# First attention pair projected before the gated part's u, wider spacing of attention pieces, squares taken from copies

## The chip, the cores and the metric

The kernel runs on one core of one Trainium2 chip. The metric is the device time of one execution in microseconds (us), as a median over runs. The core has a TensorE (matrix multiplication, in the profile PE, its weight loads PEld), a VectorE (DVE), a ScalarE (ACT), a GpSimd (POOL) and a SyncE (SP), on whose queue all loads and stores of this kernel are issued.

## The reference, cut to what matters

Two transformer blocks over 512 tokens of width 1024 in fp32: a gated delta network with a squared-ReLU MLP, and then a block whose mixer has three parts side by side. The change lies in the mixer of the second block.

```python
hn = rms_norm(h, norm1_g)
proj = hn @ w_in
a_b, a_c, a_h, q, k, v, c_u, c_v = split(proj, ...)          # 3x256, 3x512, 2x256
y_a = a_b * short_conv(a_c * a_h, conv_w)                    # gated convolution
q = rms_norm(q by head, q_norm_g); k = rms_norm(k by head, k_norm_g)   # 8 heads of 64
y_b = stick_breaking_attention(q, k, v)
y_c = gelu(c_u) * (tril(w_s) @ rms_norm(gelu(c_v)) + b_s)    # gated part, chunks of 128
h = h + concat(y_a, y_b, y_c) @ w_out
...
def stick_breaking_attention(q, k, v):                       # for each block of 128 queries
    z = q @ k.T * scale
    log_rem = where(causal, log_sigmoid(-z), 0)
    suffix = cumsum(log_rem, reverse=True) - log_rem
    o = where(causal, exp(log_sigmoid(z) + suffix), 0) @ v
```

After it come a squared-ReLU MLP and a gate with a per-layer embedding.

## The kernel before, in words

Activations lie feature-major: 128 features on the partitions, 512 tokens along the row, 8 such tiles for the width of 1024. A product in fp32 is made of three matmuls in a faster fp32 form (`mm3`, L198): the high part of the weights with the high and the low part of the activations, and the low part of the weights with the high part of the activations. Weights come in units of 128x1024 over SP's queue into two raw buffers; ScalarE makes the high part of a unit (L186) and VectorE the low part (L187). `plan` (L838) is the list of units in the order in which `take` asks for them, and two are always under way. A projection (`proj`) is 8 such triples into one PSUM tile of the two-buffer pool `mm`; all small products take theirs from the pool of six `g` buffers (`pg`).

TensorE's instructions stand in the order in which the program issues them; the instructions of the other engines are put into their queues by the scheduler of the language, except those that are pinned. The order on TensorE is made by the class `Mix`, a clock of estimated nanoseconds. Main work (projections) advances it by STEP = 655 a triple and calls `tick`, which issues each side piece (a Python generator) that has come due. A side piece gives back its own cost and the delay until it may be called again. `drain` issues all that is left, with nothing in between, and `wait` only sets the clock forward.

The mixer's stage runs so: c_v token-major (`token_major`, 256 columns); two units of c_u, whose GELU follows on ScalarE, and then a load of ScalarE's table with logarithm and exponential (pinned); the gated part (`sgu`) and the attention (`attend`) are added as sides; then the main work goes on with pair 0, 1 and 2 of q and k, V token-major, pair 3, and six projections of the gated convolution (`conv_part`); `drain`; and the output projection (L1153 on), whose TensorE work takes the attention's features last.

A pair is two heads, with one projection for q and one for k. `qk_pair` copies each to SBUF (L1120) and squares it (L1121), and adds `qk_norm`: 2500 later, sums over features on TensorE, a root on ScalarE and VectorE (L1003, L236 to L238), a way through DRAM to spread the roots over partitions (four DMAs), and 8000 after that, the scaling of q and k on VectorE (L1012). Only then is the pair `ready`. `attend` asks for that every 500, waits RD = 3500 and issues the three score pieces of each pair (`scores`, 512, 512 and 256 columns for each of the two heads). A score piece has the logits on TensorE (L1031, mask L1036), absolute value, exponential and logarithm on ScalarE (L1041 to L1043), a maximum, a running sum and a subtraction on VectorE (L1044 to L1046), and an exponential on ScalarE (L1047). One piece later its two heads are transposed on TensorE (`weights`, L1054), each copied by VectorE or ScalarE (L1057). The steps of `attend` follow each other PACE = 2370 apart, two for a score piece: one for each head. OD = 4500 after the transposes of a pair's third piece for its second head, the pair's output product (`attn_out`, L1067) falls due, half at a time. The last pair's output is in `drain`'s hands if the projections have ended by then.

Of the kernel before, what the change touches and what calls it, by code (L numbers as in the profile page):

```python
# [10 lines left out]
AF = mybir.ActivationFunctionType  # L11
# [12 lines left out]
UM = 5  # L24
UK = 3
WR = 2
PACE = 2370
OD = 4500
RD = 3500
HD = 4500  # L30
# [92 lines left out]
def tile_gdn_then_mix(ctx: ExitStack, tc: tile.TileContext, A: dict, out: bass.AP):  # L123
    nc = tc.nc
    ctx.enter_context(tc.manual_schedule(engines={mybir.EngineType.PE}))
    v, s, g, pe = nc.vector, nc.scalar, nc.gpsimd, nc.tensor
# [10 lines left out]
    mix = Mix()  # L137
# [10 lines left out]
    def us(name, shape=(P, T)):  # L148
        return up.tile(list(shape), F32, tag="us", name=name, bufs=US)
# [7 lines left out]
    def pmm(shape=(P, T), name="mm"):  # L157
        return psm.tile(list(shape), F32, tag="mm", name=name)

    def pg(shape=(P, 4, P), name="pg"):  # L160
        return psg.tile(list(shape), F32, tag="g", name=name)
# [16 lines left out]
    def wunit(ap, eng=v):  # L178
        n = ap.shape[1]
        raw = wp.tile([P, 1024], F32, tag="wr", name="wr", bufs=WR)  # L180
        nc.sync.dma_start(out=raw[:, :n], in_=ap)
        while stores:
            nc.sync.dma_start(**stores.pop(0))
        H = wp.tile([P, 1024], R, tag="wh", name="wh")
        L = wp.tile([P, 1024], R, tag="wl", name="wl")
        s.copy(H[:, :n], raw[:, :n])  # L186
        eng.tensor_tensor(out=L[:, :n], in0=raw[:, :n], in1=f(H[:, :n]), op=SUB)  # L187
        return H, L
# [15 lines left out]
    plan, asked = [], []  # L204

    def ask():
        while plan and len(asked) < 2:
            key = plan.pop(0)
            asked.append((key, wunit(A[key[0]][key[1]])))

    def take(*key):
        ask()
        k, w = asked.pop(0)
        assert k == key, (k, key)
        return w

    def proj(w_ap, xH, xL, order=range(KD), ps=None):
        H, L = w_ap
        ps = pmm() if ps is None else ps
        for i, k in enumerate(order):  # L220
            o = slice(k * P, (k + 1) * P)
            mm3(ps, H[:, o], L[:, o], xH[k], xL[k], i == 0, i == KD - 1)
            if i < KD - 1:
                mix.tick(STEP)
        mix.now += STEP
        ask()
        return ps

    def rsqrt(alloc, m, shape, pin=False):
        y0 = alloc("rs_y", shape)  # L230
        ln = s.activation(out=y0, in_=m, func=AF.Ln)
        if pin:
            tc.keep_in_program_order(ln)
        s.activation(out=y0, in_=y0, func=AF.Exp, scale=-0.5)
        t = alloc("rs_t", shape)
        v.tensor_tensor(out=t, in0=y0, in1=y0, op=MUL)  # L236
        v.scalar_tensor_tensor(out=t, in0=t, scalar=-0.5, in1=m, op0=MUL, op1=MUL)
        v.scalar_tensor_tensor(out=t, in0=t, scalar=1.5, in1=y0, op0=ADD, op1=MUL)  # L238
        return t
# [29 lines left out]
    def row_form(ps, lhs, rhs):  # L269

        for c in range(NC):
            pe.matmul(ps[32 * c:32 * c + 32], lhsT=lhs(c), rhs=rhs(c), start=True, stop=True)
        return ps
# [19 lines left out]
    def over(dst, d):  # L293
        n = dst.shape[0]
        nc.sync.dma_start(out=dst, in_=d.unsqueeze(0).to_broadcast([n] + list(d.shape)))
# [9 lines left out]
    def par(name, j=0, n=1):  # L305
        o, _ = _OFF[name]
        return prm[:, o + j:o + j + n]
# [285 lines left out]
    for m in range(31, 0, -1):  # L593
        w = 32 - m
# [226 lines left out]
    for m in range(KD):  # L821
        if m < 2:
            out_half(m, 1)
            ps = head2[m][1]
        else:
            ps = proj(wunit(A["wo"][m]), yH, yL)
# [5 lines left out]
    def mlp_plan(w1, w2):  # L832
        for half in range(2):
            plan.extend((w1, 16 * half + j) for j in range(16))
            plan.extend((w2, 4 * m + 2 * half + q) for m in range(KD) for q in range(2))

    mlp_plan("w1", "w2")
    plan += [("wcv", 0), ("wcv", 1)] + [("win2", i) for i in (0, 1, 8, 9, 10, 11, 12, 13)]  # L838
    plan += [("wv", i) for i in range(4)] + [("win2", 14), ("win2", 15)] + [("win2", 2 + i) for i in range(6)]
    plan += [("wo2", m) for m in range(KD)]  # L840
    mlp_plan("w3", "w4")
# [101 lines left out]
    def token_major(units, n, kper, fin, hook=lambda u, i: None):  # L943
        pv = [pmm((P, n), "ptm") if n == T and c < 2 else pg((P, n), "ptm") for c in range(NC)]
        for u, key in enumerate(units):
            H, L = take(*key)
            last = n == T and u == len(units) - 1
            for i in range(kper * NC):
                kk, c = (i % kper, i // kper) if last else (i // NC, (i + 2) % NC)
                k = u * kper + kk  # L950
                cs_ = slice(c * P, (c + 1) * P)
                o = slice(kk * n, kk * n + n)
                pe.matmul(pv[c], lhsT=uH[k][:, cs_], rhs=H[:, o], start=k == 0, stop=False)  # L953
                pe.matmul(pv[c], lhsT=uL[k][:, cs_], rhs=H[:, o], start=False, stop=False)  # L954
                pe.matmul(pv[c], lhsT=uH[k][:, cs_], rhs=L[:, o], start=False, stop=k == KD - 1)  # L955
                mix.tick(STEP * n // T)
                if i == kper * NC - 1:
                    ask()
                if k == KD - 1:
                    fin(c, pv[c])  # L960
                hook(u, i)
# [35 lines left out]
    def qk_norm(hp, qk, pcs):  # L997
        yield 0, SQ
        pss = pg((P, 2, P), "pss")
        for w in range(2):  # L1000
            row_form(pss[:, w], lambda c: bd[:, 48:80], lambda c: qk[:, w, c * P:(c + 1) * P])
        mq = us("mq", (P, 2, P))
        v.scalar_tensor_tensor(out=mq, in0=pss, scalar=1.0 / 64, in1=epsR.unsqueeze(1).to_broadcast([P, 2, P]), op0=MUL, op1=ADD)  # L1003
        rq = rsqrt(us, mq, (P, 2, P))
        d = dr.tile([NC, 2, 2, P], F32, name=f"rq_d{hp}")
        nc.sync.dma_start(out=d.rearrange("c e w i -> (c e) w i"), in_=rq[0:P:16])
        for e in range(2):
            for w in range(2):
                over(qk[64 * e:64 * e + 64, w].rearrange("p (c i) -> p c i", c=NC), d[:, e, w])
        yield 600, OQ  # L1010
        for w in range(2):
            v.scalar_tensor_tensor(out=qk[:, w], in0=pcs[w], scalar=(qg8, par("kg"))[w], in1=qk[:, w], op0=MUL, op1=MUL)  # L1012
        ready[hp] = (qk[:, 0], qk[:, 1])
        yield 0, 0
# [60 lines left out]
    def attend():  # L1075
        seq = [(hp, b2, e) for hp in range(4) for b2 in range(3) for e in range(2)]
        fly = []
        for i in range(len(seq) + LAG):
            cost = 0
            if i < len(seq) and seq[i][2] == 0:  # L1080
                hp, b2 = seq[i][:2]
                if b2 == 0:
                    while hp not in ready:
                        yield 0, 500
                    yield 0, RD
                fly += scores(*seq[i][:2])
                yield fly[-1][-1] * 5 // 3, GAP
            if i >= LAG:
                w = fly.pop(0)
                weights(*w)  # L1090
                cost += w[-1] * 5 // 6
                if w[1:3] == (2, 1):
                    mix.add(attn_out(w[0]), OD)
            yield cost, max((PACE if seq[min(i, len(seq) - 1)][2] else PACE - GAP) - cost, 300)

# [18 lines left out]
    def qk_pair(hp):  # L1114
        qk = k4("qk", shape=(P, 2, T))
        pcs = []
        for w in range(2):
            ps = proj(take("win2", 8 + 2 * hp + w), uH, uL)
            pc = um("pc")
            s.copy(pc, ps)  # L1120
            s.activation(out=qk[:, w], in_=ps, func=AF.Square)  # L1121
            pcs.append(pc)
            mix.tick(0)
        mix.add(qk_norm(hp, qk, pcs), 0)

    nrm = norms()
    token_major([("wcv", i) for i in range(2)], 256, 4, cv_done, lambda u, i: next(nrm) if (u, i) in ((0, 10), (1, 11)) else None)
    for m in range(2):
        ps = proj(take("win2", m), uH, uL)
        mix.tick(0)  # L1130
        t = um("t")
        v.tensor_tensor(out=t, in0=ps, in1=rcB, op=MUL)
        s.activation(out=cu[:, m], in_=t, func=AF.Gelu)
# [2 lines left out]
    mix.add(sg, next(sg)[1])  # L1136
    rc2 = uk("rc2")
    g.tensor_tensor(out=rc2, in0=rcB, in1=rcB, op=MUL)
    mix.add(attend())
    qk_pair(0)  # L1140
    qk_pair(1)
    qk_pair(2)
    token_major([("wv", i) for i in range(4)], 512, 2, v_done)
    done.add("V")
    qk_pair(3)
    conv_part(0)
    conv_part(1)
    mix.drain()
# [4 lines left out]
    for m in range(KD):  # L1153
        scale_h(m)
        ps = proj(take("wo2", m), yH, yL, (0, 1, 6, 7, 2, 3, 4, 5))
# [20 lines left out]
    for m in range(KD):  # L1176
# [11 lines left out]
        if m < KD - 1:  # L1188
            ps = proj(take("wg", m), uH, uL, ps=pg((P, T), "mm") if m < 2 else None)
# [4 lines left out]
        for c in (slice(0, 256), slice(256, 512)):  # L1194
            ps = pmm((P, 256), "mmh")
# [98 lines left out]
```

## Time and profile before

| | |
|---|---|
| Median of 3 runs | 1284.78 us (1284.68 to 1289.81) |
| Profiled execution | 1285.04 us |
| Its span | 1282.9 us, 16468 instructions |
| PEld | 1039.4 us (81%) |
| DVE | 733.9 us (57%) |
| ACT | 545.6 us (43%) |
| POOL | 118.2 us (9%) |
| DMA | 132.07 MB, mean 103 GB/s |

The span is the time from the first to the last profiled instruction. Shares are busy time over the span. TensorE's matmuls are pipelined: a matmul's row is longer than the distance to the next one's start (0.39 against 0.23 us for 512 columns), so TensorE's pace is read from starts, and an idle time is counted only where nothing was in flight. TensorE's clock was granted in full in all 40 slices of the page.

### The profile page before, as it was taken

What the parts mean: (1) busy time and instruction counts of PE and PEld (TensorE: products, weight loads), DVE (VectorE), ACT (ScalarE), POOL (GpSimd) and SP (SyncE); (2) the same over time, 40 slices, a digit from 0 to 9 for tenths busy, and PEclk for the clock granted to TensorE, in tenths of its full rate; (3) what the DMA queues carried; (4) which work ended last, traced back from release to release, by engine and by line L of the source; (5) the groups of instructions that cost most, each with busy time, mean ns of one, the idle gap of its engine ahead of it and who ended that gap; (6) DMA issues with size and microseconds to landing.
All of it is one profiled execution on the core that took longest, in us unless ns stands there. A gap on an engine that the chain in (4) does not pass through costs nothing.

```text
span 1282.9 us, 16468 instructions
## 1 busy us (share of the span) xinstructions
PE 1269.6 (99%) x6440; PEld 1039.4 (81%) x6440; DVE 733.9 (57%) x1048; ACT 545.6 (43%) x1018; POOL 118.2 (9%) x115
## 2 busy tenths in 40 slices
PE   9999999999999999999999999999999999999998
PEld 6878878898888888888888766678888888888887
DVE  5898987765444333444445686866444334444445
ACT  5876534564344112443334566643332113333332
POOL 1224000002100110000222000012000110000100
PEclk9999999999999999999999999999999999999999
DMA  5332432353333233333333331323333333333343
GB/s 175 108 99 75 128 119 67 107 173 99 107 94 92 94 99 99 99 99 99 99 124 101 100 99 51 83 82 107 107 99 99 93 93 95 97 99 99 99 148 114
DMA packets 51476, 132.07 MB, mean 103 GB/s; under 512 B 4852, under 2 KB 17992, under 8 KB 51400
## 3 DMA queue, kind: packets, MB, share of 16 engines
q1 hardware_dynamic: 51400, 131.04, 33.5%
q8 instruction: 50, 0.82, 0.3%
q14 instruction: 26, 0.21, 0.1%
HBM read 124.67 MB, written 6.35 MB: 102 GB/s over the span
## 4 chain that ended last, share of the span: by engine, by line
PE 85%; DVE 7%; ACT 3%; issue 2%; DMA 1%; POOL 1%; SPq 0%; POOLq 0%; DVEq 0%; ACTq 0%
PE mm L199 25%; PE mm L200 25%; PE mm L201 25%; DVE u L465 1%; DVE wl L187 1%; DVE Xd L598 1%; PE pz L1031 1%; DVE bs L596 1%; DMA eg<-cum_d 1%; PE ptm L953 1%; PE po L1067 1%; PE ptm L955 1%; PE ptm L954 1%; PE pwt L1054 1%; PE po L783 1%
## 5 line engine op out<-in xcount | busy, mean ns | idle before, releaser
L187 DVE TENSOR_TENSOR wl<-wr,wh 128x1024 fp32r<-128x1024 f32 x206 | 271.2, 1316 | 263.6 <-ACT wh L186 262.9
L186 ACT CAST wh<-wr 128x1024 fp32r<-128x1024 f32 x206 | 217.1, 1054 | 465.2 <-PE mm L200 380.1
L199 PE MATMUL mm<-fH,wh 128*128 128x512 f32 x512 | 199.2, 389 | 0.0
L200 PE MATMUL mm<-fL,wh 128*128 128x512 f32 x512 | 199.2, 389 | 0.0
L201 PE MATMUL mm<-fH,wl 128*128 128x512 f32 x512 | 199.2, 389 | 0.0
L199 PEld LDWEIGHTS mm<-fH,wh 128*128 128x128 f32 x512 | 96.1, 188 | 20.0
L201 PEld LDWEIGHTS mm<-fH,wl 128*128 128x128 f32 x512 | 96.1, 188 | 20.0
L200 PEld LDWEIGHTS mm<-fL,wh 128*128 128x128 f32 x512 | 96.1, 188 | 19.8
L199 PE MATMUL mm<-xH,wh 128*128 128x512 f32 x256 | 106.7, 417 | 1.2 <-ACT xH L167 1.0
L201 PE MATMUL mm<-xH,wl 128*128 128x512 f32 x256 | 100.3, 392 | 0.5 <-DVE wl L187 0.5
L200 PE MATMUL mm<-xL,wh 128*128 128x512 f32 x256 | 100.2, 391 | 0.3 <-DVE xL L173 0.3
L199 PE MATMUL mm<-x1H,wh 128*128 128x512 f32 x256 | 99.7, 389 | 0.0
L199 PE MATMUL mm<-x2H,wh 128*128 128x512 f32 x256 | 99.7, 389 | 0.0
L201 PE MATMUL mm<-x1H,wl 128*128 128x512 f32 x256 | 99.6, 389 | 0.0
L201 PE MATMUL mm<-x2H,wl 128*128 128x512 f32 x256 | 99.6, 389 | 0.0
L200 PE MATMUL mm<-x1L,wh 128*128 128x512 f32 x256 | 99.6, 389 | 0.0
L200 PE MATMUL mm<-x2L,wh 128*128 128x512 f32 x256 | 99.6, 389 | 0.0
L876 DVE TENSOR_TENSOR t<-mm,rr 128x512 f32<-128x512 f32 x32 | 22.1, 692 | 107.5 <-PE mm L201 107.5
L167 ACT ACTIVATE fH<-t 128x512 fp32r<-128x512 f32 x64 | 40.5, 632 | 89.7 <-DVE t L864 89.7
L171 DVE TENSOR_TENSOR fL<-t,fH 128x512 fp32r<-128x512 f32 x64 | 44.3, 692 | 44.7 <-ACT fH L167 44.7
L199 PEld LDWEIGHTS mm<-xH,wh 128*128 128x128 f32 x256 | 48.2, 188 | 13.8 <-ACT xH L167 2.3
L201 PEld LDWEIGHTS mm<-xH,wl 128*128 128x128 f32 x256 | 48.0, 188 | 11.4 <-DVE wl L187 1.0
(331 smaller groups left out, 2207.8 us busy)
## 6 DMA issues: line engine op xcount, KB each, us to landing
wr<-in_w SPq DMA_DIRECT2D x128, 512.0 KB, 3.5
wr<-in_wqkv SPq DMA_DIRECT2D x22, 512.0 KB, 3.7
wr<-in_wo SPq DMA_DIRECT2D x16, 512.0 KB, 3.5
wr<-in_win SPq DMA_DIRECT2D x16, 512.0 KB, 3.6
wr<-in_wgate SPq DMA_DIRECT2D x8, 512.0 KB, 4.2
wr<-in_wg SPq DMA_DIRECT2D x8, 512.0 KB, 3.4
x<-in_xT SPq DMA_DIRECT2D x8, 256.0 KB, 5.4
eg<-cum_d SPq DMA_DIRECT2D x8, 256.0 KB, 5.7
```

Source lines behind the costliest of these rows:

```text
L167: i = s.activation(out=H, in_=src, func=AF.Copy, scale=scale)
L171: eng.tensor_tensor(out=L, in0=src, in1=f(H), op=SUB)
L186: s.copy(H[:, :n], raw[:, :n])
L187: eng.tensor_tensor(out=L[:, :n], in0=raw[:, :n], in1=f(H[:, :n]), op=SUB)
L199: pe.matmul(ps, lhsT=wH, rhs=xH, start=first, stop=False)
L200: pe.matmul(ps, lhsT=wH, rhs=xL, start=False, stop=False)
L201: pe.matmul(ps, lhsT=wL, rhs=xH, start=False, stop=last)
L465: v.scalar_tensor_tensor(out=u[:, d:], in0=t[:, :T - d], scalar=w(3 - d), in1=u[:, d:], op0=MUL, op1=ADD)
L596: v.tensor_tensor(out=t, in0=Z[:, m, 0:m].unsqueeze(2).to_broadcast([P, m, w]), in1=Xd[:, m, m:32].unsqueeze(1).to_broadcast([P, m, w]), o ...
L598: v.tensor_tensor(out=Xd[:, 0:m, m:32], in0=Xd[:, 0:m, m:32], in1=t, op=SUB)
L783: pe.matmul(po[:, j], lhsT=QK.chunks(h)[:, c], rhs=y[:, j], start=not c, stop=True)
L876: v.tensor_tensor(out=t, in0=ps, in1=rr, op=MUL)
```

## The change

The attention's PACE goes from 2370 to 2950. The two units of pair 0 stand ahead of the two units of c_u in the plan, and pair 0 is projected ahead of c_u. `qk_pair` now returns its norm instead of adding it; pair 0's is added behind c_u, the table load and the start of the gated part, just before the attention; the others' are added where they were. The square is taken from the SBUF copy and no longer from PSUM.

```diff
-PACE = 2370
+PACE = 2950
...
-    plan += [("wcv", 0), ("wcv", 1)] + [("win2", i) for i in (0, 1, 8, 9, 10, 11, 12, 13)]
+    plan += [("wcv", 0), ("wcv", 1)] + [("win2", i) for i in (8, 9, 0, 1, 10, 11, 12, 13)]
...
             s.copy(pc, ps)
-            s.activation(out=qk[:, w], in_=ps, func=AF.Square)
+            s.activation(out=qk[:, w], in_=pc, func=AF.Square)
             pcs.append(pc)
             mix.tick(0)
-        mix.add(qk_norm(hp, qk, pcs), 0)
+        return qk_norm(hp, qk, pcs)
...
     token_major([("wcv", i) for i in range(2)], 256, 4, cv_done, lambda u, i: next(nrm) if (u, i) in ((0, 10), (1, 11)) else None)
+    norm_0 = qk_pair(0)
     for m in range(2):
         ps = proj(take("win2", m), uH, uL)
...
     g.tensor_tensor(out=rc2, in0=rcB, in1=rcB, op=MUL)
+    mix.add(norm_0)
     mix.add(attend())
-    qk_pair(0)
-    qk_pair(1)
-    qk_pair(2)
+    mix.add(qk_pair(1))
+    mix.add(qk_pair(2))
     token_major([("wv", i) for i in range(4)], 512, 2, v_done)
     done.add("V")
-    qk_pair(3)
+    mix.add(qk_pair(3))
```

## Rows read from the trace of the kernel before

**Rows 1.** The page's table of engines: busy us, share, instructions.
```profile
PE 1269.6 (99%) x6440; PEld 1039.4 (81%) x6440; DVE 733.9 (57%) x1048; ACT 545.6 (43%) x1018; POOL 118.2 (9%) x115
```
**Rows 2.** Waits of TensorE: who for whom, us in total, times, longest.
```profile
PE ptm L953 <- ACT qk L1121: 1.7, 1, 1.7
...
PE pz L1031 <- issue: 1.1, 1, 1.1
...
PE pz L1031 <- DVE a L1046: 0.8, 1, 0.8
...
PE ptm L955 <- DVE wl L187: 0.4, 1, 0.4
```
**Rows 3.** Windows of the mixer's stage: stretch, length, busy us by engine, clock, DMA.
```profile
673.70:841.31 167.61, 163.60 (x931) 122.39 (x930) 119.15 (x184) 100.05 (x187) 9.76 (x6) 1.00 0.30 86
```
**Rows 4.** Timeline of TensorE in that stage: start, length, what.
```profile
727.42 1.13 PE L1031 MATMUL pz<-qk 64*128 64x512 f32 x4
...
818.86 1.14 PE L1031 MATMUL pz<-qk 64*128 64x128 f32 x8
...
827.41 1.08 PE L1031 MATMUL pz<-qk 64*128 64x256 f32 x4
...
837.30 0.38 PE L1054 MATMUL pwt<-ident,a 128*128 128x128 f32 x2
...
839.00 2.38 PE L1067 MATMUL po<-wT,Vt 128*64 128x512 f32 x16
841.31 0.50 PE L199 MATMUL mm<-y2H,wh 128*128 128x512 f32 x1
```
**Rows 5.** Timeline of ScalarE in that stage.
```profile
741.17 0.61 ACT L1121 ACTIVATE qk<-mm 128x512 f32<-128x512 f32 x1
...
820.90 1.07 ACT L1041 ACTIVATE a<-pz 128x512 f32<-128x512 f32 x2
...
827.71 1.23 ACT L1047 ACTIVATE a<-a 128x512 f32<-128x512 f32 x2 [2.24 <-DVE a L1046]
...
829.31 0.66 ACT L1041 ACTIVATE a<-pz 128x256 f32<-128x256 f32 x2
...
833.21 0.75 ACT L1047 ACTIVATE a<-a 128x256 f32<-128x256 f32 x2
...
837.72 0.37 ACT L1057 COPY wT<-pwt 128x256 f32<-128x256 f32 x1 [2.19 <-PE pwt L1054]
```
**Rows 6.** Timeline of VectorE in that stage.
```profile
703.53 3.04 DVE L187 TENSOR_TENSOR wl<-wr,wh 128x1024 fp32r<-128x1024 f32 x1 [2.50 <-ACT wh L186]
...
725.53 0.74 DVE L1012 SCALAR_TENSOR_TENSOR qk<-pc,prm,qk 128x512 f32<-128x512 f32 x1
...
810.50 0.75 DVE L1012 SCALAR_TENSOR_TENSOR qk<-pc,prm,qk 128x512 f32<-128x512 f32 x1
...
823.56 1.29 DVE L1044 SCALAR_TENSOR_TENSOR a<-pz,a 128x512 f32<-128x512 f32 x2 [0.89 <-ACT a L1043]
...
827.01 1.26 DVE L1046 TENSOR_TENSOR a<-pz,a 128x512 f32<-128x512 f32 x2
```
**Rows 7.** Timeline of POOL: the second product of the gated part's norm.
```profile
703.09 2.40 POOL L982 TENSOR_TENSOR sgc<-sgc 128x1024 f32<-128x1024 f32 x1
```
**Rows 8.** Groups of ScalarE by form: squares from SBUF and from PSUM.
```profile
L246 ACT ACTIVATE sq<-h 128x512 f32<-128x512 f32 x28 | 17.5, 625 | 9.6 <-DVE h L877 9.6
...
L1121 ACT ACTIVATE qk<-mm 128x512 f32<-128x512 f32 x8 | 4.8, 605 | 0.0
```
**Rows 9.** TensorE's first matmuls, and windows behind its last one (clock: third from last).
```profile
5.66 0.80 PE L199 MATMUL mm<-xH,wh 128*128 128x512 f32 x1
...
7.06 0.39 PE L199 MATMUL mm<-xH,wh 128*128 128x512 f32 x1
...
1278.40:1282.90 4.50, 0.00 (x0) 0.00 (x0) 1.24 (x3) 0.42 (x1) 0.00 (x0) 1.00 0.12 40
1282.90:1284.00 1.10, 0.00 (x0) 0.00 (x0) 0.00 (x0) 0.00 (x0) 0.00 (x0) 0.61 0.05 15
```

## The prediction

> **What bounds the kernel now.** I read the page's table of engines first: TensorE is busy for 1269.6 of 1282.9 us [rows 1], so only what it stands still for can be won, and only what makes it stand still can be lost. TensorE's waits, in its own list, come next. Four of them lie between 736 and 812 us, in the stage that the change touches: 1.7 us for the square of k of pair 2 (L1121), 1.1 put down to "issue", 0.8 for a subtraction of the attention (L1046), 0.4 for a weight's low part (L187) [rows 2]. The windows say the same from the other side: from the first matmul of c_v (673.7) to the first of the output projection (841.31), TensorE is busy for 163.60 of 167.61 us [rows 3]. The whole stake on the winning side is therefore 4.0 us, or 0.31%. Last I read the timelines of TensorE, ScalarE, VectorE and POOL around those waits and at the stage's end [rows 4 to 7].
>
> **The order that the planner writes.** TensorE runs in the order of the program, and that is made by the Mix clock. I worked its list through by the costs and delays in the code, counting from c_v. For the old kernel the four pairs begin their scores at 49.5, 72.3, 95.3 and 118.2 (thousand units), and the projections end at 141.6. The trace confirms it piece by piece: between pair 3's third score piece (827.41) and its last transposes (837.30) the list puts 3, 1, 3 and 4 triples around the other transposes, and after them two triples before the output matmuls at 839.00; the starts agree [rows 4]. For the new kernel the same list gives 47.6, 73.6, 100.5 and 127.4. Pair 0 doesn't get ahead by a projection's length, since its norm is only added behind u: it starts where it did, less the 1.8 that the two gated pieces cost while pair 0 was projected. PACE then adds 0.58 to each of 6 steps, 3.5 a pair, and from pair to pair 26.0 to 26.9 instead of 22.9. Pair 3's second score piece now comes behind the sixth triple of the last projection, and the projections end at 139.5. Behind them, with nothing left to put between, come five of pair 3's six transposing pieces, its third score piece and its output. The planner's own waits there cost no time; the data's do.
>
> **The costs, part by part.**
>
> The four waits. The subtraction's wait (0.8) came where a score piece followed too closely: each holds its PSUM until its first subtraction, some 8.8 us (818.86 to 827.6) [rows 4, 6]. The new list puts 9.7 us of TensorE's work between the two. The "issue" wait (1.1) is pair 3's q and k, scaled only by 811.25 [rows 6]; the new list asks for them 9 us later. The weight's low part sat behind pair 0's first piece on VectorE, which now is 1.9 us earlier. These go: -2.3. The square's wait: TensorE went on at 741.83, just behind the square (741.17, 0.61 long) [rows 5]; the copy ends 0.5 earlier, and ScalarE's queue ahead of it starts 1.9 earlier. It keeps between 0 (queue earlier) and 1.2 (only the square gone); I take 0.4. Together -3.6.
>
> The squares from copies. 8 squares at 625 ns instead of 605, the two groups nearest [rows 8], and none overlaps its own copy any more, some 0.1 each: about 1 us of ScalarE over 150, hidden by TensorE's projections; should that cover be gone, it is at most 0.15 per square.
>
> Pair 0 earlier. The same 48 matmuls and four DMAs in another place. The two weight loads change places in SP's queue, and none is added. The copies of pair 0 are held some 11 us longer, two of five buffers of that kind; u's two are freed before pair 1's second copy wants one. Nothing: 0.
>
> Pair 0's norm beside the gated part. The gated part's two POOL products ran at 701 to 705.5, before any norm. With u moved by two projections (10.9 us) they run at 712 to 716.4, which is where pair 0's norm runs on VectorE. In this trace a VectorE subtraction issued at 703.53 under POOL's 2.40 us product ended only at 706.57, 1.08 after POOL, so it lost 1.96 [rows 6, 7]. Pair 0's q and k are ready at 726.27 for scores at 727.42 [rows 4, 6], a slack of 1.15. One such block leaves a wait of 0.8, none leaves 0, both products some 3. I take 0.8.
>
> The Trainium skill (SBUF — State Buffer, "Who interferes with whom") has the two engines share one port pair as an exclusive lock, for VectorE operations with two SBUF inputs against a reading POOL. By that rule the three small products of the norm's root are blocked and the first step, which reads PSUM, isn't; the sum is then 4.0 below, and without the rule it would be 3.2. The row agrees for the weight's subtraction; for the small products no row shows it.
>
> The end of attention. Call the start of pair 3's second score piece X. Old: X = 818.86; its absolute values began at 820.90, behind two exponentials that ended at 821.0; its two subtractions ran 827.01 to 828.27, its exponentials ended at 828.94, X + 10.1 [rows 4 to 6]. With pieces spaced wider that queue is gone: X + 9.5. The third piece took from 829.31 to 833.96 on ScalarE and VectorE, 4.65 [rows 5]; with one copy of 0.5 between, X + 14.6. From the last transposes (837.30) to the end of their copy (838.09) is 0.8: X + 15.4. The output matmuls take 2.31 (839.00 to 841.31): X + 17.7. The last projection ends at X + 5.5 (1.3 of its own, two triples of 0.68, pair 2's output 2.31, one transposing piece 0.5). So 12.2 us pass between the last projection and the output projection, against 5.4 us of work that was done between projections before (a transposing piece 0.5, two of 0.45, two of 0.25, the third score piece 1.2, the output 2.3). New idle: 6.8. From below: were the third piece's PSUM free at once and VectorE without a gap (823.56 to 828.27 for the second piece, 4.7, and half of that for the third, which is half as wide), X + 14.8, 3.9 idle. From above: the gated conv's last products and splits, the earlier copies and a weight's low part, 3 us together, all ahead of it on VectorE: 9.8.
>
> Sum: -3.6 + 0.8 + 6.8 = +4.0 us. The profiled execution took 1285.04 us (span 1282.9 and 2.1 around it), 0.26 above the median of 1284.78; the median becomes 1288.8.
>
> **The rivals.**
>
> A, the tail hides. If the three engines drain pair 3 as fast as its pieces come, the waits won stand alone: -3.6, 1281.2. For it: ScalarE and VectorE are half idle on average. Against it: the chain of one piece is 9.5 us long whatever the average, and the list leaves 5.5.
>
> B, the clock falls in the tail (the other side). Place: between the second piece's last transposes (X + 9.9) and the third's (X + 14.3) TensorE issues nothing for 4.4 us, after 2 us of the same. It decides if the granted clock falls before the output matmuls. At the start a 512-column matmul took 0.80 us where the same took 0.39 two microseconds later [rows 9], the levels of 1.2 and 2.4 GHz; the slow start reached past 5.66. Price: half of 5.7 us, 2.8: 1291.6, slower than before by 0.53%. Against: idle for 4.5 us behind its last matmul, TensorE still had 1.00, and fell only in the next window [rows 9]. The skill (TensorE: Matmul & The Clock Gate, "HAM oscillation") has idle gaps bring the throttled state back; by that rule B is what happens.
>
> C, the lock costs more. Both POOL products block the norm: 3 us instead of 0.8, 1291.0. For it: they run back to back. Against: only one wait of that kind in this stage, and POOL may be the one that waits.
>
> D, the queues at the end. The upper bound of 9.8 idle: 1291.8. For it: ScalarE and VectorE run their queues in order, and the last conv products fall into the same 12 us. Against: in the old run they lay between pieces without delaying one.
>
> **How the numbers follow.** The forecast 0.58, A 0.08, B 0.18, C 0.06, D 0.10. What a measurement can tell from no change is about 0.5%, 6.4 us. Faster by that asks for more than the stage's whole idle: 0.02. Slower (above 1291.2): half of B, most of D, a third of C and the upper edge of the forecast, 0.24. The rest, 0.74, is no difference. The bounds together span -0.1 to +10.0; for 8 in 10 I take 1284.4 to 1292.4, which leaves out A and the worst sums.
>
> **What would show it.** TensorE's waits: the square, the subtraction and the "issue" wait gone or below 0.5; new ones of 6 to 7 us in all in one place, before pair 3's last transposes and the second half of its third score piece, on ScalarE's exponential (L1047) and VectorE's subtraction (L1046). The gap between the last uH matmul and the first of the output projection is about 12 us instead of 2.3. A wait of about 0.8 at pair 0's first scores. The granted clock at 1.00 throughout, else B. I am wrong if projections still stand between pair 3's last pieces, or if the four waits stay.

## The result: 0.9% slower, and the profile after

The changed kernel takes 1297.96 us (median of 6, 1296.04 to 1300.29) against 1286.69 for the kernel before on the same chip (median of 6, 1284.68 to 1289.81): a ratio of 1.0089, 95% interval 1.0079 to 1.0100. The forecast was 1288.8, and its range ended at 1292.4. The profiled execution took 1298.21 us (span 1296.1), 13.17 above the profiled one of before.

The page's table of engines, after, against [rows 1]:

```profile
PE 1275.0 (98%) x6440; PEld 1042.7 (80%) x6440; DVE 734.7 (57%) x1048; ACT 546.1 (42%) x1018; POOL 119.4 (9%) x115
```

TensorE has the same 6440 instructions and is busy 5.4 us longer: something made the same matmuls slower. The windows say where. They list stretch and length, busy us (with count) of PE, PEld, DVE, ACT and POOL, then the granted clock, the DMA share and GB/s. The first row is the mixer's stage, from the first matmul of c_v to the first of the output projection; the other two are the stretches at half rate in it.

```profile
674.20:854.50 180.30, 168.92 (x931) 125.29 (x929) 120.26 (x184) 100.70 (x187) 10.72 (x6) 0.95 0.27 83
727.86:731.28 3.42, 3.13 (x22) 1.30 (x22) 0.23 (x1) 0.73 (x2) 0.00 (x0) 0.50 0.40 147
840.50:854.15 13.65, 9.15 (x30) 5.26 (x31) 8.24 (x16) 5.78 (x15) 0.00 (x0) 0.50 0.10 38
```

Against [rows 3] the stage is 12.69 us longer, which is nearly all of the difference. 5.32 of it is longer busy time (168.92 less 163.60), the price of TensorE at 1.2 GHz for 3.4 and 13.65 us. The other 7.37 is standing still: 11.38 us now, 4.01 before. TensorE's list of waits (who for whom, us in total, times, longest) gives the pieces of the 11.38:

```profile
PE pwt L1054 <- ACT a L1047: 3.9, 2, 3.5
PE pz L1031 <- DVE a L1046: 2.6, 1, 2.6
PE pz L1031 <- DVE qk L1012: 2.4, 1, 2.4
...
PE mm L199 <- DVE tc L1103: 1.1, 1, 1.1
...
PE ptm L953 <- ACT pc L1120: 0.8, 1, 0.8
...
PE mm L199 <- DVE yc L1111: 0.7, 1, 0.7
```

All of [rows 2] is gone or has become a smaller one: the square of k is now a wait of 0.8 for its copy. The first two lines are the end of attention, the third is pair 0's first scores. The two on `mm` are the first two projections of the second convolution part (they start at 813.13 and 820.05): each waits until VectorE has read a product of the first part (`tc`, `yc`) out of the PSUM buffer that it is to fill.

The timeline of TensorE at those places (start, length, engine, line, what; in brackets the idle time before and its releaser), which answers to [rows 4]:

```profile
728.15 2.15 PE L1031 MATMUL pz<-qk 64*128 64x512 f32 x4 [2.38 <-DVE qk L1012]
...
831.64 1.14 PE L1031 MATMUL pz<-qk 64*128 64x128 f32 x8
...
837.29 0.60 PE L1054 MATMUL pwt<-ident,a 128*128 128x128 f32 x4
837.82 0.70 PE L1031 MATMUL pz<-qk 64*128 64x256 f32 x2
841.09 1.19 PE L1031 MATMUL pz<-qk 64*128 64x256 f32 x2 [2.57 <-DVE a L1046]
...
848.06 0.69 PE L1054 MATMUL pwt<-ident,a 128*128 128x128 f32 x2 [3.45 <-ACT a L1047]
...
849.78 4.79 PE L1067 MATMUL po<-wT,Vt 128*64 128x512 f32 x16
854.50 0.50 PE L199 MATMUL mm<-y2H,wh 128*128 128x512 f32 x1
```

Pair 0's first scores take 2.15 us instead of 1.13, and the last output matmuls 4.79 instead of 2.38: both run at half rate, each behind a wait. With X = 831.64, the start of pair 3's second score piece, the last projection ends at X + 5.65 and the output projection starts at X + 22.86. All that lies between is attention with no projection beside it, as the worked-out list had it.

Why pair 0's q and k come late is seen on VectorE (against the second row of [rows 6], k's scaling at 725.53) and on POOL:

```profile
712.56 0.42 DVE L1003 SCALAR_TENSOR_TENSOR mq<-pss,sgc 128x256 f32<-128x256 f32 x1 [0.26 <-PE pss L272]
713.92 0.65 DVE L236 TENSOR_TENSOR rs_t<-rs_y 128x256 f32<-128x256 f32 x1 [0.94 <-ACT rs_y L234]
714.61 2.52 DVE L237 SCALAR_TENSOR_TENSOR rs_t<-rs_t,mq 128x256 f32<-128x256 f32 x1
717.16 0.42 DVE L238 SCALAR_TENSOR_TENSOR rs_t<-rs_t,rs_y 128x256 f32<-128x256 f32 x1
...
724.94 0.75 DVE L1012 SCALAR_TENSOR_TENSOR qk<-pc,qg,qk 128x512 f32<-128x512 f32 x1 [2.26 <-DMA qk<-rq_d]
725.61 1.22 DVE L187 TENSOR_TENSOR wl<-wr,wh 128x1024 fp32r<-128x1024 f32 x1
726.74 0.69 DVE L171 TENSOR_TENSOR y2L<-t,y2H 128x512 fp32r<-128x512 f32 x1
727.35 0.75 DVE L1012 SCALAR_TENSOR_TENSOR qk<-pc,prm,qk 128x512 f32<-128x512 f32 x1
```

```profile
712.38 1.91 POOL L979 TENSOR_TENSOR sgc<-cvu,rs_t 128x1024 f32<-128x1024 f32 x1 [19.34 <-DVE rs_t L238]
714.37 2.47 POOL L982 TENSOR_TENSOR sgc<-sgc 128x1024 f32<-128x1024 f32 x1
```

The product of the root that was issued at 714.61, beside POOL's second product, took 2.52 us and ended 0.3 us behind it; before, beside nothing on POOL, the same instruction took 0.42. Its neighbour at 713.92, beside the end of POOL's first product, took 0.65 for 0.43, while `mq`, which reads PSUM and one SBUF tile, wasn't held at all. That is what the Trainium skill (SBUF — State Buffer, "Who interferes with whom") says of an exclusive port pair, and the trace agrees on each of the three. It is called the lock here. Then comes a second delay. Between q's scaling and k's stand a weight's low part and a split; the two scalings start 2.41 us apart, and 0.67 before, so this costs 1.7 us. Before, the two scalings stood back to back (q's here, k's at 725.53 in [rows 6]):

```profile
716.52 0.42 DVE L238 SCALAR_TENSOR_TENSOR rs_t<-rs_t,rs_y 128x256 f32<-128x256 f32 x1
...
724.86 0.75 DVE L1012 SCALAR_TENSOR_TENSOR qk<-pc,qg,qk 128x512 f32<-128x512 f32 x1 [0.82 <-DMA qk<-rq_d]
```

### The profile page after: what moved, and what is told of

It is laid out like the page before. It is cut to its first block, busy times and chain, and to the rows that moved or that the text cites. A ratio compares the mean times of both kernels' runs of the same rounds, so it can differ in the third digit from the quotient of the medians.

```text
span 1296.1 us, 16473 instructions
## 1 busy us (share of the span) xinstructions
PE 1275.0 (98%) x6440; PEld 1042.7 (80%) x6440; DVE 734.7 (57%) x1048; ACT 546.1 (42%) x1018; POOL 119.4 (9%) x115
```

## The experiments

The first batch takes the change apart. The second takes away the two causes that the traces then named, one at a time and together. The third adds a control. Medians of one batch share their runs of before, and the median of before lies between 1285.72 and 1286.69 from batch to batch, so runs of different batches are compared by their ratios. The start of c_v, which none of the edits touches, lies between 673.3 and 676.6 in the twelve profiles, so effects under 2 us are read from the stage and not from the span.

**Spacing alone** (the kernel before, with one constant changed):

```
-PACE = 2370
+PACE = 2950
```

> The kernel before with PACE 2950 alone (order and squares as before). Theory: the spacing makes the tail. By the planner's list pair 3's second score piece is now issued just behind the last projection, so its whole chain lies open: the changed kernel took 22.9 us from that piece's start to the output projection, here nearly all of it uncovered, less some 9.5 us of TensorE's own work, plus the halved clock while TensorE idles; against the waits that wider spacing takes away (2 to 3). I expect 9 to 12 us over before, no wait at pair 0's first scores, and a clock fall at the end. Rival (the new order of pair 0 and u makes the loss): within 3 us of before.

Measured: 1294.16, ratio 1.0061 (1.0047 to 1.0075). TensorE's waits:

```profile
PE pwt L1054 <- ACT a L1047: 5.3, 2, 4.1
...
PE pwt L1054 <- DVE a L1046: 2.2, 1, 2.2
PE ptm L955 <- DVE wl L187: 1.9, 1, 1.9
```

The stage takes 176.27 us. The tail is there without the new order, with half rate in it:

```profile
841.69:851.93 10.24, 6.12 (x20) 4.21 (x22) 6.91 (x14) 4.24 (x12) 0.00 (x0) 0.50 0.00 0
```

Two waits come up in the middle as well, and behind the one of 2.2 us (it ends at 748.98) the clock is at 0.50 from 749.52 to 752.93. The size, 8.4 us by the medians, is just under the 9 to 12 that were expected.

**Order alone** (the changed kernel, with spacing and squares as they were):

```
-PACE = 2950
+PACE = 2370
...
-            s.activation(out=qk[:, w], in_=pc, func=AF.Square)
+            s.activation(out=qk[:, w], in_=ps, func=AF.Square)
```

> The changed kernel with PACE 2370 and squares from PSUM again, so the order alone. Theory: a wait of 2.4 us at pair 0's first scores (the norm's root blocked behind POOL) and 1.6 of halved clock behind it, no tail (the list still has projections between pair 3's last pieces): 2 to 5 us over before, VectorE's root product under POOL's second product again near 2.5 us. Rival (the order makes the whole loss): 9 to 12 over. Second rival (all of it is spacing): within 1 us.

Measured: 1299.77, ratio 1.0104 (1.0088 to 1.0121), no better than the whole change (by the medians 14 us over before, by the ratio 13; the two intervals overlap). That went against my theory. The stage takes 179.53 us, against 180.30.

```profile
PE pz L1031 <- DVE qk L1012: 5.1, 2, 2.8
PE ptm L955 <- DVE wl L187: 2.4, 1, 2.4
...
PE pwt L1054 <- DVE a L1046: 1.9, 1, 1.9
```

There is no tail. Pair 0's scores wait 2.31, behind the same product of the root (2.51 us here). At the old spacing the earlier pair 0 also puts the pieces of all pairs earlier, and they catch up with q's and k's norms: pair 3's scores wait 2.81. VectorE's queue shows one such place:

```profile
763.08 0.75 DVE L1012 SCALAR_TENSOR_TENSOR qk<-pc,qg,qk 128x512 f32<-128x512 f32 x1 [6.81 <-DMA qk<-rq_d]
```

q's scaling of pair 2 stands at the head of the queue for 6.81 us waiting for its DMA, and pair 1's pieces and a weight's low part stand behind it; TensorE then waits 2.43 for that low part. Three times in this stage the clock falls to half rate for 3.41 us each (from 730.10, 771.06 and 822.26). So +8 and +13 alone make +11 together: with the wider spacing the waits that the order brings in the middle don't come up (but for pair 0's), and the tail does.

**Squares alone** (the kernel before, `in_=pc` for `in_=ps`):

> The kernel before with the squares taken from the copies alone. Theory: the 1.7 us wait of TensorE for k's square before V becomes one for the copy and shrinks by 0.5 to 1.0, nothing else moves: 0.3 to 1.0 us under before, within what can be measured. Rival (the square's longer SBUF read and the lost overlap on ScalarE cost time): 0 to 2 over.

Measured: 1285.23, ratio 0.9996 (0.9986 to 1.0005); the stage 167.31 us instead of 167.61. The wait of 1.7 for the square has become one of 1.2 for the copy. Costing these squares at nothing was right: by their group they take 638 ns instead of the 605 of [rows 8].

**Filling the tail** (the changed kernel, with matmuls of ones that nothing reads, 12 calls ahead of pair 3's third score piece and 14 ahead of its last transposes):

```
+    def keep_clock(n):
+        pf = pmm((P, 256), "pfill")
+        for _ in range(n):
+            pe.matmul(pf, lhsT=ones..., rhs=ones..., start=True, stop=True)
...
+        if (hp, b2) == (3, 2):
+            keep_clock(12)
...
+        if (hp, b2, e) == (3, 2, 0):
+            keep_clock(14)
```

> The changed kernel with 12 matmuls of ones by ones into an unread PSUM buffer ahead of pair 3's third score piece and 14 ahead of its last transposes, in time in which TensorE stood still. Theory: idle TensorE lets the granted clock fall at 840.5, and the output matmuls run at half speed (4.7 us instead of 2.3); with the fill the clock stays at 1.00 there and the time falls by 2 to 4 us. Rival (the tail is the data's chain alone and the clock does not matter): no change, or up to 1 us more for the added matmuls.

Measured: 1297.52, ratio 1.0091 (1.0076 to 1.0106). The clock stays up in the tail (1.00 from 842 to 856 us), but the fill takes 5.39 and 6.26 us there, longer than the waits of 2.57 and 3.45 that it replaced. And behind the wait at pair 0's first scores, which the edit doesn't touch, the half rate lasted 6.82 us here instead of 3.42. This run decides nothing.

**Fill of the right size** (6 and 8 calls instead):

> After, with 6 calls of a 256-column fp32 matmul of ones put on TensorE ahead of pair 3's third score piece and 8 ahead of its last transposes (0.427 us a call at full clock: 2.6 and 3.4 us in place of the 3.0 and 3.5 us in which TensorE stood still). Theory, half of the tail's price is the clock: with the fill no fall in the tail, the last output matmuls take 2.3 to 2.6 us instead of 4.72, and the end comes 2 to 3.5 us earlier, 1294.5 to 1296. Rival, the chain alone sets the end and the clock only slows work that waits anyway: no change from after, within 0.7 us.

Measured: 1297.25, ratio 1.0085 (1.0073 to 1.0097). The clock is up, and the last output matmuls show it:

```profile
833.11 1.14 PE L1038 MATMUL pz<-qk 64*128 64x128 f32 x8
...
850.69 2.90 PE L1076 MATMUL po<-wT,Vt 128*64 128x512 f32 x16
853.52 0.50 PE L199 MATMUL mm<-y2H,wh 128*128 128x512 f32 x1
```

Pair 3's second score piece starts at 833.11, so the output projection comes at X + 20.41 instead of X + 22.86. The stage is 1.94 us shorter (178.36). The median moved by 0.7 only, and the intervals of the two ratios overlap: by the times the rival holds, and the profile shows a gain at the lower end of what was expected.

**The lock taken away** (the changed kernel; the gain of the gated part's norm is no longer multiplied in on POOL, but per partition, in VectorE's sum with the bias):

```
-        g.tensor_tensor(out=vn4, in0=vn4, in1=gv..., op=MUL)
...
-            v.tensor_tensor(out=t, in0=psv, in1=bB[:, pr]..., op=ADD)
+            v.scalar_tensor_tensor(out=t, in0=psv, scalar=par("sg", pr), in1=bB[:, pr]..., op0=MUL, op1=ADD)
```

> After, with the gain of the gated part's norm moved off GpSimd: its product there (L982, 2.47 us) is dropped, and the gain is applied on VectorE in the sum with the bias that stands there anyway (L992, a scalar_tensor_tensor in place of a tensor_tensor). Theory, the lock: VectorE's second refinement of pair 0's root (L237, 2.52 us beside that product, 0.42 by median) gets about 2 us shorter, so the wait at pair 0's first scores falls from 2.4 to 0.5 us or less, TensorE's clock no longer falls behind it (3.41 us at half rate in after), and the end comes 3 to 4 us earlier: 1294 to 1295, the tail's idle time and its half clock unchanged. Rival, the queue on VectorE and the two DMAs of the row form alone: the wait stays at 1.5 us or more, the fall of the clock with it, and the time within 1 us of after.

Measured: 1294.08, ratio 1.0067 (1.0054 to 1.0080). On VectorE, the product that took 2.52 us, and the scalings:

```profile
713.23 0.65 DVE L236 TENSOR_TENSOR rs_t<-rs_y 128x256 f32<-128x256 f32 x1 [0.93 <-ACT rs_y L234]
713.92 0.43 DVE L237 SCALAR_TENSOR_TENSOR rs_t<-rs_t,mq 128x256 f32<-128x256 f32 x1
...
723.06 0.75 DVE L1011 SCALAR_TENSOR_TENSOR qk<-pc,qg,qk 128x512 f32<-128x512 f32 x1 [1.01 <-DMA qk<-rq_d]
723.73 1.22 DVE L187 TENSOR_TENSOR wl<-wr,wh 128x1024 fp32r<-128x1024 f32 x1
```

It takes 0.43 now, while its neighbour, still beside POOL's first product (711.70 to 713.60), again takes 0.65: the lock is shown. The wait at pair 0's scores is 1.2, not the 0.5 that I expected; the weight's low part and the split still stand between the scalings, and the DMAs between root and scaling took 8.25 us here against 7.36 in the changed kernel. The clock no longer falls there. The stage is 3.03 us shorter, and by its windows 2.92 of that is busy time:

```profile
673.52:850.79 177.27, 166.00 (x931) 124.03 (x929) 118.48 (x184) 100.68 (x187) 8.15 (x5) 0.97 0.29 84
839.77:850.01 10.24, 5.94 (x18) 3.29 (x20) 6.17 (x13) 4.62 (x13) 0.00 (x0) 0.50 0.18 51
```

The 1.2 us that the first scores gained in waiting were given back in three later waits by 0.2 to 0.5 each. What remained of the gain is clock: no half rate at the scores, and 10.24 us of it in the tail instead of 13.65.

**Spacing for each pair** (the changed kernel; from pair 1 on, every piece stands behind the same projection matmul as before):

```
-PACE = 2950
+PACE = (2700, 2400, 2100, 2000)
...
-            yield cost, max((PACE if seq[...][2] else PACE - GAP) - cost, 300)
+            hp, _, e = seq[...]
+            yield cost, max((PACE[hp] if e else PACE[hp] - GAP) - cost, 300)
```

> After, with a spacing for each pair, 2700, 2400, 2100 and 2000, instead of 2950 for all: the new order and the squares stay, and from pair 1 on every attention piece stands behind the same projection matmul as in before, the last transposes behind the sixth group of the last convolution projection. Theory, the spacing alone makes the tail (6.5 us idle and its half clock): both go, and 2.4 us of wait at pair 0's first scores with its fall of the clock (about 2) stay: 1287 to 1290. Rival, the order itself moves the chains against each other wherever the pieces stand (as the order alone at the old spacing cost 13): waits of 2 us or more come up in the middle, and the time stays at 1293 or more.

Measured: 1290.85, ratio 1.0036 (1.0024 to 1.0049), 0.85 above the end of what was expected. The tail is gone with its waits and those of the convolution's projections; what stays is the wait at pair 0's scores, with a longer fall behind it, as the windows and the longest of its waits there show, and 3.4 us of smaller waits (the longest 1.2, for a weight's low part).

```profile
673.28:845.76 172.48, 166.23 (x931) 123.55 (x929) 118.80 (x183) 100.06 (x187) 10.09 (x6) 0.98 0.27 83
727.16:733.98 6.82, 6.32 (x29) 3.62 (x30) 2.12 (x5) 3.46 (x7) 0.00 (x0) 0.50 0.29 79
```

```profile
PE pz L1031 <- DVE qk L1012: 2.8, 1, 2.8
```

**Both** (the last two edits together):

> The last two edits together: the gain off GpSimd, and the spacing for each pair. Theory, the lock and the spacing account for the whole loss: 1284 to 1286.5, no fall of TensorE's clock in the stage, idle time in the stage back to 4 to 5 us. Rival, a remainder is left that belongs to the order (pair 0 earlier), by waits that neither edit touches: 1288 or more.

Measured: 1286.81, ratio 1.0007 (0.9999 to 1.0016).

```profile
675.22:843.23 168.01, 163.01 (x930) 121.82 (x929) 117.08 (x183) 100.12 (x187) 7.56 (x5) 1.00 0.29 85
```

```profile
PE mm L201 <- DVE wl L187: 1.8, 2, 1.3
...
PE ptm L953 <- ACT pc L1120: 1.2, 1, 1.2
...
PE pz L1030 <- DVE a L1045: 0.9, 1, 0.9
PE pwt L1053 <- ACT a L1046: 0.9, 1, 0.9
...
PE pz L1030 <- DVE qk L1011: 0.4, 1, 0.4
```

This is 0.3 above the end of what was expected. No fall of the clock, 5.00 us of idle time, and a stage 0.4 us above that of before. The lock (with what it sets off) and the wide spacing account for the loss to within about 1 us (0.9 by the ratio, and at most 2.1 by its interval). What they leave of the new order is other waits, 5.00 us in all where there were 4.01: no gain over the kernel before. The spacing that does this isn't the old one but one fitted to each pair; the order at the old spacing with the lock taken away was not run.

**Lock and fill together:**

> After, with the gain off GpSimd and the right-sized fill (6 and 8 calls) together. Theory, the two act at different places and add: the gain alone took 3.9 us off the time, the fill alone 2.4 us off the stretch from pair 3's second score piece to the output projection (22.9 to 20.4 us), though its median came out only 0.7 lower; together, TensorE's clock falls nowhere in the stage, that stretch takes 20.4 us again, and the end comes at 1291 to 1292.5. Rival, the clock costs nothing in the end (the fill alone showed its real worth by its median): 1293.4 or more.

Measured: 1293.66, ratio 1.0054 (1.0042 to 1.0066).

```profile
675.11:850.56 175.45, 169.50 (x958) 127.82 (x957) 118.24 (x184) 100.76 (x187) 8.70 (x5) 1.00 0.29 85
```

The second score piece starts at 830.15, so the output projection again comes at X + 20.41. The clock is at 1.00, and the busy time, less about 6.1 of fill (28 matmul records, 0.218 us apart), is 163.4, that of before. The stage is 1.82 shorter than with the lock alone taken away; the median is 0.4 lower, the mean of the spans of its runs 1.2, and by the ratios, each against the runs of before of its own batch, the gain is 1.7 us, with intervals that overlap. By its median the rival holds, by the stage and the ratio the theory. Its c_v began 1.6 us later than in the other's profile, which hides most of the gain in the profiled spans.

**Control** (the kernel before, with the gain off POOL):

> Control: the kernel before, with only the gain off GpSimd. Theory, the lock matters only where pair 0's norm is moved beside GpSimd's products: no change, within 1 us of before (its products there fall beside nothing that the projections wait for). Rival, the edit is worth 3 to 4 us by itself, whatever the order: 1282 to 1283.

Measured: 1286.47, ratio 1.0002 (0.9993 to 1.0010).

```profile
703.28 1.23 DVE L187 TENSOR_TENSOR wl<-wr,wh 128x1024 fp32r<-128x1024 f32 x1 [2.51 <-ACT wh L186]
```

This subtraction, which took 3.04 us in [rows 6], now takes 1.23: the same lock, seen in the kernel before too, where nothing waited for it. It had cost 1.8 us there (the prediction's 1.96 took 1.08 for the subtraction alone). It costs time only where something late is behind it.

## Why the prediction was wrong, step by step

The sum was +4.0 and the stage shows +12.7: -3.2 for the old waits (4.01 to 0.77), +2.4 at pair 0's scores, +1.75 at the convolution's projections, +6.5 of idle time in the tail, +5.3 of clock.

- The four old waits, -3.6 with 0.4 left: right. 0.8 is left.
- Squares from copies, 0: right, by their own run.
- The planner's list: right. Counted from c_v's start, pair 0 asks for its scores 2.1 us earlier than before (728.15 less the wait of 2.38 and 674.20, against 727.42 less 673.70), where 1.8 was worked out, and no projection stands between pair 3's last pieces.
- **Pair 0's norm beside the gated part, +0.8: mis-sized by 1.6.** The lock was there, at one product and a little at another, 2.3 us in all where 1.96 was taken. The slack of 1.15 to set against it was read from the end of k's scaling, with both scalings back to back. In the new order other work came between the two, 1.7 us of it. Lock and queue make 4.0, less 0.6 for DMAs that were faster this time (7.36 us against 7.92), less the slack: about 2.3, and 2.4 was measured. Rival C had the size (3 us), but by both POOL products, and it was one product and a queue.
- **The waits at the convolution's projections, +1.75: not in the sum.** VectorE reads `tc` (812.40) and `yc` (819.22) late, among the second and third score pieces of pair 2. Such crowding was foreseen only in rival D, at the end, as a delay to the attention and not to the projections. With the narrower spacing the waits are gone, and with the spacing alone or the order alone they don't come up either: they need both.
- The tail, 6.8 of new idle time: 6.48 measured, yet the output projection came at X + 22.86 and not at X + 17.7. The chain was 2.7 us longer to the output matmuls (X + 18.14 against X + 15.4). Of that, 1.9 lies in the third piece, which took 6.6 us on ScalarE and VectorE from its first absolute value to its last exponential, where 4.65 was taken: an exponential and a copy of the second piece stood between its steps in ScalarE's queue, the convolution's last split and a copy in VectorE's. Another 0.9 is that it began at X + 10.9 and not at X + 10.0. ScalarE's first and last instruction of that piece:

```profile
842.53 0.38 ACT L1041 ACTIVATE a<-pz 128x256 f32<-128x256 f32 x1 [0.93 <-PE pz L1036]
...
848.70 0.42 ACT L1047 ACTIVATE a<-a 128x256 f32<-128x256 f32 x1 [0.69 <-DVE a L1046]
```

The output matmuls then took 2.4 more. The idle time agrees because the slower matmuls fill a part of the longer chain; the right number stands for a wrong length.
- **The clock, 0 in the sum: the step that failed most, 5.3 us.** It was rival B at 0.18 and 2.8 us, for the tail alone. The argument against it was the clock at 1.00 for 4.5 us behind the last matmul of the kernel [rows 9]. That row shows one fall that came late and says nothing of a fall that comes early (and its two matmuls at the start lie 1.4 us apart, not two). In the changed kernel the clock fell at 727.86, in the wait of 2.38 us, and at 840.50, in the one of 2.57. The Trainium skill (TensorE: Matmul & The Clock Gate, "HAM oscillation") has idle gaps bring the throttled state back, and here the trace agrees, at two places and not at one, and for gaps of 2.38 and 2.57 us, shorter than those of the section's example. By an estimate, half of 3.13 us of busy time at the first place is 1.6, and the other 3.7 is the tail's. With the lock taken away, and so without the fall at the first place, 2.92 us of busy time went (in that run the fall in the tail was shorter too). How much of the tail's part reaches the end is settled less well: 0.4 to 0.7 us by the medians of the two fills of the right size, 0.5 and 1.7 by the ratios, 1.8 and 1.9 by the stage, 2.4 by the stretch from X. Within one kernel the spans go along with the clock: the six of the changed kernel are 1293.9 and 1294.6 us at a mean granted clock of 0.994, 1295.6 and 1298.0 at 0.992, and 1296.1 and 1298.2 at 0.991. That doesn't part the clock from the waits that bring it down.

So the direction of the sum was right, and its two costly places too, and its size was a third of the real one. Of the 8.7 us that it lacks in the stage 5.3 are the clock, because each of two waits was priced as a wait, while each also slowed the matmuls behind it; 1.6 are pair 0's norm and 1.75 the projections of the convolution. B, C and D came true in part and together; the range held each of them alone.

## What to carry to other kernels

Price a new wait of TensorE with the half-rate matmuls that may follow it (here behind waits of 2.38 and 2.57 us), at every place and not only at the longest. When work is moved, read what the in-order queues will hold between its own steps, and what POOL runs beside it. Spacing the pieces of a pipeline wider moves its last pieces beyond the work that covers them, so the spacing belongs to the stretch where a wait is seen.

## What I had not expected of the hardware

- A fall of the clock behind a single wait was over after 3.41 us in some runs (the changed kernel's first scores, three times in the order alone) and after 6.82 in others at the same first scores (the spacing for each pair, the first fill). In the order alone it came only when TensorE worked again: the wait ended at 729.03, the clock fell at 730.10, and the first scores still ran at the full rate (1.20 us). In the tail, where more waits followed, the half rate lasted 10.24 to 13.65 us, and it was still there when the output matmuls ran.
- The DMAs that spread pair 0's root took 7.24 to 8.25 us from the end of the root to q's scaling in seven profiles, which is nearly as much scatter as the slack of 1.15 that stood against it.
